# Five edits to the order of a one-core decoder trunk: a bias tile moved to another slot, and work queued behind query splits, a first cast and the last sums

## The chip, the cores and the metric

The kernel runs on one core of a Trainium2 chip. The metric is the device time of one execution in microseconds (us); lower is better. Five engines work side by side, each in its own order: TensorE (PE) multiplies, VectorE (DVE) and ScalarE (ACT) do elementwise work, GpSimd (POOL) does a little of it, SyncE (SP) mostly issues DMA transfers.

## The reference, cut to what matters

One layer of a decoder for 1024 prompt tokens and 64 sample tokens (8 sequences of 8), model width 1024, all in fp32:

```
mod = silu(c) @ ada_w + ada_b;  shift, scale, gate = split(mod, 3)
h   = rmsnorm(x, norm_g) * (1 + scale) + shift
z   = h @ w_in + b_in                      # a_u a_v a_g | b_q b_k b_v b_g | c_... | m_g
ya  = chunk_gmlp(a_u, a_v, ...) * silu(a_g)
q, k = rmsnorm(b_q, qn_g), rmsnorm(b_k, kn_g)          # per head of 64
yb  = sliding_window_attention(q, k, b_v, sinks) * silu(b_g)
yc  = mlstm(...) * silu(c_g)
merged = sum over br of sigmoid(m_g[br]) * (y[br] @ w_branch[br])
out = x + gate * (merged @ w_out)
```

## The kernel before

Each fp32 operand of a matmul is split into a high part (a cast to fp32r, on ScalarE) and a low part (operand minus high part, on VectorE), and three products are summed: high x high, high x low, low x high. So nearly every weight block costs a DMA, a cast on ScalarE and a subtraction on VectorE before TensorE may use it. The tokens are cut into nine tiles (eight of 128 prompt tokens, one of 64 sample tokens) or into two halves of 544.

The order within an engine is made by a planner that simulates the program: each engine's queue is fixed before the run, and an instruction that must wait holds up all behind it on that engine. `tc.issue_after(ins)` makes instructions of a block stand behind `ins` in the queue of `ins`'s engine; it sets an order and adds no semaphore. From the attention on, TensorE's queue is the program's order (`manual_schedule`). SBUF is handed out by name: `slot("m1", ...)` is a fixed region that passes from one user to the next, and a pool tile (`bt(...)`) takes memory that earlier phases used. A new user waits for the old one's last reader.

The phases, in order of time:

1. Start (to about 75 us): four blocks of the modulation are multiplied (`mod`, steps M0 to M3). Each ends in a copy of a PSUM bank to `msb` (ScalarE, L356), which small matmuls with `sel` then read. Then `hprep` makes the activations `hh`, `hlo`. Step P, the last, loads and splits the second weight slab (`load_pieces(1)`, four casts L124 and four subtractions L125); its VectorE part stands behind the last `modB` of M3.
2. Branch C (to about 353 us), whose results `hn[h]` lie in the slots m0 to m3, are gated there (L799) and stored (`dy<-hn`, on POOL's queue).
3. Attention (to about 600 us). `kv_tile` computes keys and values tile by tile; VectorE adds the bias tile `bkb` and so frees the PSUM bank (L942, L943). `bkb` lies in the memory of the later tile `Pp`. The first sums `t_first` (four times two subtractions, a sum and a split over 128x544) are issued among the kv tiles. A list of steps then runs the queries: `Prompt.q` computes the norms of three query tiles at a time (`q_stats`: squares L1001, row sums L1002, and on POOL a power L163) and then transposes and splits one tile (`q_transpose`: cast L1027, subtraction L1028); two steps later `s` does the logits and the softmax, two more later `p` transposes the probabilities `Sm`. Other products (queries, gMLP rows, gates) fill in. `t_second(k)` and `t_third(0)` make further sums; `mix(g)` is the last use of the slots y7, m5, y6, m0.
4. Products of halves (to about 1070 us): `items` is a list of pairs (prepare, run). `prepare` loads and splits a weight block up to LEAD = 5 items ahead, `run` multiplies. The first four are gMLP blocks of `plain`, (i, j) = (0,0), (0,1), (1,0), (1,1): its first run needs (0,0) and (0,1). `splits[n]` holds the cast and the subtraction of the n-th split made there. `last_gate`, `t_late(k)` and `t_in_place(k)` stand between them.
5. Projections and output. `proj` loads the earlier partial sum (`mprev<-dmg`, SP) and adds it; for f = 3 and 7 `m_split` splits the finished sum into `mh`, `ml` at once (L1643, L1644). The output product reads `mh`, `ml` and the output weights, loaded by `wo_load(0)` to `wo_load(3)` (each eight DMAs, four casts, four subtractions).

Of the kernel before, what the change touches and what calls it, by code (L numbers as in the profile page):

```python
# [8 lines left out]
F32 = mybir.dt.float32  # L9
# [18 lines left out]
HT = NT // 2  # L28
# [10 lines left out]
def trunk_kernel(ctx: ExitStack, tc: tile.TileContext, I, O):  # L39
# [197 lines left out]
    with tc.tile_pool(name="start", bufs=1, side="right", reuse_waits="tile") as st:  # L237
# [110 lines left out]
        def mod(j):  # L348
            pm = pk()
            for q in range(4):  # L350
                o = slice(256 * (q // 2), 256 * (q // 2) + 256)
                for kk in range(4):
                    mm(pm[32 * kk:32 * kk + 32, o], sT[:, 4 * (q % 2) + kk], ada_raw[j, q][:, 256 * kk:256 * kk + 256],
                       q % 2 == 0, q % 2 == 1)
            msb = st.tile([128, 512], F32, tag="msb", bufs=2, name="msb")
            S.copy(msb, pm)  # L356
            pc = pk()
            if j == 0:
                tr(pc[:, 128:160], Ra)
                V.tensor_copy(cols[:, CADA:CADA + 32], pc[:, 128:160])  # L360
                V.tensor_scalar(cols[:, CADA + 8:CADA + 16], cols[:, CADA + 8:CADA + 16], 1.0, None, ALU.add)
            for q in range(4):
                mm(pc[:, 16 * q:16 * q + 9], msb[:, 128 * q:128 * q + 128], sel, True, True)
            for d in range(2):
                k = 2 * j + d
                last["m"] = V.tensor_scalar(modA[:, k], pc[:, 16 * d:16 * d + 9], cols[:, CADA + 8 + k:CADA + 9 + k],
                                cols[:, CNG + k:CNG + k + 1], ALU.add, ALU.mult)
                V.tensor_scalar(modB[:, k], pc[:, 32 + 16 * d:32 + 16 * d + 9], cols[:, CADA + k:CADA + k + 1],
                                None, ALU.add)
# [37 lines left out]

        for step in STEPS.split():
            if step == "P":
                with tc.issue_after(last["m"].ins):  # L410
                    load_pieces(1, [None] * 3 + [st.tile([128, 528], F32, name="raw1")])
            elif step == "S":
                ps = pk()
                tr(ps[:, 0:68], R1)
                V.tensor_copy(cols[:, 0:CADA], ps[:, 0:CADA])
                V.tensor_copy(cols[:, CCB:100], ps[:, CADA:68])
            elif step[0] == "N":
                norm(int(step[1]))
            elif step[0] == "M":
                mod(int(step[1]))  # L420
            else:
                ci = int(step[2])
                for k in range(int(step[0]), int(step[1]) + 1):
                    hprep(k, ci)
                    for i in range(2 if ci < 2 else 1):
                        part(k, ci, i)
# [402 lines left out]
        t_split(x, to[0][:, c], to[1][:, c])  # L829
        TT[q, k] = to  # L830

    T4S = ("y6", "m0", "m4", "m1")

    kept = []
    keep = ExitStack()
# [2 lines left out]
    with tc.tile_pool(name="bph", bufs=1, side="right", reuse_waits="tile") as b1:  # L838
        def bt(shape, name, dt=F32, bufs=1, tag=None):
            return b1.tile(shape, dt, tag=tag or name, bufs=bufs, name=name)  # L840

        bkb = bt([128, 256], "bkb", tag="Pp")
        nc.sync.dma_start(bkb, b_in[:, 2048:2304].broadcast_to([128, 256]))
        qgb = bt([128, 64], "qgb")
        nc.sync.dma_start(qgb, I["swa_qnorm_g"].broadcast_to([128, 64]))
# [164 lines left out]
                    V.tensor_tensor(qr, qr, r3[:64, 2, 2 * i:2 * i + 2].unsqueeze(2).broadcast_to([64, 2, 64]), ALU.mult)  # L1010


        def q_transpose(g, n):
            tn = TILES[n][1]
            pq = pk()
            for i in range(2):
                tr(pq[:, tn * i:tn * i + tn], qraw[g][i][:tn, n])
            QT = bt([128, 2, 2, 128], "QT", F32R, bufs=3) if n < 8 else bt([128, 8, 4, 8], "QTs", F32R, bufs=2)
            for r in range(2):
                a, b = slice(64 * r, 64 * r + 64), slice(64 - 64 * r, 128 - 64 * r)  # L1020
                if n < 8:
                    src = pq[a, 0:256].rearrange("p (i t) -> p i t", i=2)
                    hi, lo = QT[a, :, r], QT[b, :, r]
                else:
                    src = pq[a, 0:128].rearrange("p (i b t) -> p b i t", i=2, b=8)
                    hi, lo = QT[a, :, r::2], QT[b, :, r::2]
                S.copy(hi, src)  # L1027
                V.tensor_tensor(lo, src, hi.bitcast(F32), ALU.subtract)  # L1028
            return QT.rearrange("p i r t -> p (i r t)")


# [2 lines left out]
        class Prompt:  # L1034
# [2 lines left out]

            def q(self):
                g, n = self.g, self.n
                if n % 3 == 0:  # L1040
                    q_stats(g, n)
                self.rr = r3s[g][:, n % 3]
                self.QT = q_transpose(g, n)
                if n == 7:
                    QTs[g] = q_transpose(g, 8)

# [185 lines left out]

        def t_second(k):
            x = slot(("m1", "m1", "y2", "y3")[k], [128, HT], name="tx")
            t_next(x, 6, k, k + 4, 1, 5, t_tile(("y0", "y1", "m2", "m3")[k]), slice(0, HT))

        def t_third(k):
            to = t_tile(T4S[k])
# [51 lines left out]
        def seq(*fs):  # L1290
# [2 lines left out]
        tail = {11: lambda: t_second(0), 13: lambda: t_second(1), 17: lambda: t_second(2),  # L1293
                18: seq(lambda: t_second(3), a_norm, lambda: a_scale(0)), 19: lambda: a_scale(1), 20: seq(lambda: a_scale(2), a_load),
                21: seq(lambda: a_scale(3), lambda: mix(0)), 22: seq(lambda: mix(1), lambda: mix(2)),
                23: lambda: mix(3), 24: lambda: t_third(0)}

        hl = next_slab()
        for n in range(9):
# [225 lines left out]
    def plain(cols2, final):  # L1525

        st = {}

        def prep(i, j):
            return w_split(raw_load(kv(w_in[:, cols2[i]:cols2[i] + 128])[:, 4 * j:4 * j + 4]))  # L1530

        def run(i, h):
            for j in range(2):
                c = part_(h, j)
                ps = bank()[:, :CUT[j][1]]
                for k in range(8):
                    three(ps, st[i, k // 4], k % 4, hh[k][:, c], hlo[k][:, c], k == 0, k == 7)
                x = tt(j)
                with tc.high_priority():
                    S.copy(x, ps)  # L1540
                final(i, h, j, x)

        def first(i, j, t):
            st[i, j] = t
            if j:
                run(i, 1)

        out = [(lambda i=i, j=j: prep(i, j), lambda t, i=i, j=j: first(i, j, t)) for i in range(2) for j in range(2)]
        return out + [(None, lambda _, i=i: run(i, 0)) for i in range(2)]

    Q7 = (1, 6, 7, 5, 3, 2, 4)
# [82 lines left out]
                V.tensor_tensor(yl[f][:, c], x, yh[f][:, c].bitcast(F32), ALU.subtract)  # L1634

    mh, ml = [None] * 8, [None] * 8

    def m_tiles(f):
        mh[f] = hp.tile([128, 1152], F32R, tag=f"hh{f}", name="mh")
        ml[f] = hp.tile([128, NT], F32R, tag=f"hl{f}", name="ml")  # L1640

    def m_split(f, c0, n, x):
        S.copy(mh[f][:, c0:c0 + n], x)  # L1643
        V.tensor_tensor(ml[f][:, c0:c0 + n], x, mh[f][:, c0:c0 + n].bitcast(F32), ALU.subtract)  # L1644
        if c0 + n == NT:
            S.copy(mh[f][:, NT:1152], ml[f][:, 1024:NT].bitcast(F32))

    def proj(n, f, Tt):
        br = ORDER_BR[n]

        def prep():
            return w_split(raw_load(kv(I["w_branch_" + "abc"[br]][0][:, 128 * f:128 * f + 128])))

        def run(t):
            if n == 2 and f % 4 == 3:
                m_tiles(f)
            for h in range(2):
                for j in range(2):
                    c = part_(h, j)
                    x = Tt[f, h, j]  # L1660
                    ps = bank()[:, :CUT[j][1]]
                    for k in range(4):
                        three(ps, t, k, yh[k][:, c], yl[k][:, c], k == 0, k == 3)
                    prev = None
                    if n:
                        prev = mp(CUT[j][1], "mprev")
                        nc.sync.dma_start(prev, dmg[f, :, c])
                    with tc.high_priority():
                        V.scalar_tensor_tensor(x, x, 1.0, ps, ALU.add, ALU.mult)
                    if n:  # L1670
                        V.tensor_tensor(x, x, prev, ALU.add)
                    if n == 2 and f % 4 == 3:
                        m_split(f, c.start, CUT[j][1], x)
                    else:
                        nc.sync.dma_start(dmg[f, :, c], x)

        items.append((prep, run))
# [37 lines left out]
    def last_gate(_):  # L1715
        c0, n, ps = kept[0]
        tz = y2[0].tile([128, 2, HT], F32, tag="yh1", name="tz")
        t, z = tz[:, 0, :n], tz[:, 1, :n]
        with tc.issue_after(splits[1][0]), tc.issue_after(splits[1][1]):
            S.activation(t, ps[:, :n], AF.Tanh, bias=bh[:, CBG + 3:CBG + 4], scale=0.5)  # L1720
            S.activation(z, ps[:, :n], AF.Identity, bias=cols[:, CBG + 3:CBG + 4], scale=1.0)
            V.scalar_tensor_tensor(z, t, 1.0, z, ALU.add, ALU.mult)
# [2 lines left out]
    it = [plain((0, 1024), gmlp_pair(0))]  # L1725
    it += [seven((128 * g, 1024 + 128 * g), (1, 2, 5, 6, 3, 7, 4) if g == 1 else Q7, gmlp_pair(g)) for g in range(1, 4)]
    gr = [x for g in range(4) for x in gate_rows(g)]
    items += [(None, last_gate)] + it[0][:2] + [behind(t_late, 1, 1)] + it[0][2:4] + [behind(t_late, 3, 2, 3), act(t_in_place, *((k,) for k in range(4)))] + it[0][4:]
    rest = it[1][:2] + [None] + it[1][2:3] + [None] + it[1][3:4] + [None] + it[1][4:5] + [None] + it[2][:1] + [None]
    rest += it[1][5:6] + [None] + it[1][6:] + [None] + it[2][1:2] + [None] + it[2][2:] + it[3]  # L1730
    items += [x or gr.pop(0) for x in rest]
# [33 lines left out]
        items[i][1](ready.pop(i))  # L1765


    gbc = slot("m6", [128, 1024], name="gbc")
    gbs = slot("m7", [128, 1024], name="gbs")
    nc.sync.dma_start(gbc, drow[0:1].broadcast_to([128, 1024]))  # L1770
# [23 lines left out]
    wo_load(0)  # L1794
    for i in range(4):
        if i < 3:
            wo_load(i + 1)
        c = slice(256 * i, 256 * i + 256)
        for n in tuple(range(9)) if i < 3 else (8,) + tuple(range(8)):
            t0, tn = TILES[n]  # L1800
# [55 lines left out]
```

## Time and profile before

| | |
|---|---|
| median of 3 runs | 1200.13 us (1199.48 to 1201.68) |
| profiled execution: its own time | 1201.65 us |
| profiled execution: span, first to last instruction | 1199.9 us |
| TensorE busy | 1160.6 us (97% of the span) |
| VectorE, ScalarE, GpSimd busy | 775.9, 489.0, 82.3 us |
| mean granted TensorE clock | 0.991 |

The span is shorter than the execution's own time by what lies before the first and after the last instruction. Busy time counts an engine's own instructions; matmuls overlap, so a busy TensorE need not be at its peak.

### The profile page before, as it was taken

The numbers are of one execution on the slowest core, as the hardware profiler recorded it, in microseconds if no ns is written. First come the engines' busy times: TensorE is split into PE (matmuls) and PEld (weight loads), VectorE is DVE, ScalarE is ACT, GpSimd is POOL, SyncE is SP. The second block draws the span as 40 slices with busy tenths as digits, with TensorE's granted clock in tenths as the row PEclk, the third lists the DMA queues.
The fourth block names the chain that finished last, engine by engine and source line by source line (L and its number), as shares of the span: only waits on it lengthen the run. The fifth ranks groups of instructions, "written<-read, shape, count | busy, mean of one in ns | idle before, by whom it ended". The sixth has DMA issues, their size and how long they took to land.

```text
span 1199.9 us, 23127 instructions
## 1 busy us (share of the span) xinstructions
PE 1160.6 (97%) x8924; PEld 1112.5 (93%) x8924; DVE 775.9 (65%) x1846; ACT 489.0 (41%) x1225; POOL 82.3 (7%) x111
## 2 busy tenths in 40 slices
PE   5899999999998999999999999999999999999998
PEld 2699999999988998888898999999999999998998
DVE  2577877655466678786588983645766676668333
ACT  4543455444332277887343441324332343335000
POOL 2100011012023210010000000000000000000000
PEclk9999999999998999999999999999999999999999
DMA  9721222222221210212234256423543354475322
GB/s 310 237 83 36 74 65 82 86 79 94 89 83 50 73 40 25 71 41 88 67 104 143 63 156 190 132 78 114 165 117 108 110 165 110 127 232 180 94 90 73
DMA packets 150772, 129.73 MB, mean 108 GB/s; under 512 B 13613, under 2 KB 140213, under 8 KB 150648
## 3 DMA queue, kind: packets, MB, share of 16 engines
q1 hardware_dynamic: 142984, 118.96, 33.4%
q0 software_dynamic: 2240, 7.08, 1.7%
q10 hardware_dynamic: 5440, 2.23, 0.7%
q8 instruction: 70, 1.15, 0.4%
q14 instruction: 38, 0.31, 0.1%
HBM read 99.39 MB, written 29.82 MB: 108 GB/s over the span
## 4 chain that ended last, share of the span: by engine, by line
PE 87%; DMA 5%; DVE 4%; SPq 3%; ACT 1%; issue 1%; ACTq 0%; DVEq 0%
PE pg L85 49%; PE pk L85 22%; PE pu L85 13%; PE pk L89 2%; DMA adaraw<-in_ada_w_dram 2%; SPq L251 1%; PE pu L89 1%; DMA mrow<-in_ada_b_dram 1%; DMA raw<-in_w_in_dram 1%; DMA mgr<-dmg 1%; DMA gbs<-drow 0%; SPq L267 0%; DMA raw<-in_w_out_dram 0%; DVE hl L125 0%; DVE wo L1395 0%
## 5 line engine op out<-in xcount | busy, mean ns | idle before, releaser
L85 PE MATMUL pg<-hl,hl 128*128 128x256 f32 (+3 forms) x904 | 279.2, 309 | 0.8 <-DVE hl L389 0.8
L85 PE MATMUL pg<-hh,hl 128*128 128x384 f32 (+1 forms) x912 | 238.1, 335 | 2.9 <-DVE hh L388 1.2
L85 PE MATMUL pg<-hl,hh 128*128 128x256 f32 (+1 forms) x1008 | 180.4, 286 | 5.3 <-DVE vB L943 5.3
L85 PEld LDWEIGHTS pg<-hl,hl 128*128 128x128 f32 x904 | 171.9, 190 | 3.9 <-DVE hl L389 1.7
L85 PEld LDWEIGHTS pg<-hh,hl 128*128 128x128 f32 x912 | 161.8, 189 | 7.4 <-DVE hh L388 2.6
L85 PEld LDWEIGHTS pg<-hl,hh 128*128 128x128 f32 x1008 | 152.5, 191 | 5.7 <-issue 5.4
L1394 ACT CAST prod<-raw 128x512 fp32r<-128x512 f32 x77 | 47.4, 619 | 118.6 <-PE pk L85 50.2
L85 PE MATMUL pg<-hh,prod 128*128 128x288 f32 (+1 forms) x408 | 86.9, 293 | 1.8 <-ACT prod L1394 1.6
L85 PE MATMUL pk<-hh,prod 128*128 128x256 f32 (+1 forms) x400 | 80.9, 285 | 0.0
L85 PEld LDWEIGHTS pg<-hh,prod 128*128 128x128 f32 x408 | 68.2, 191 | 2.7 <-ACT prod L1394 1.9
L1556 ACT ACTIVATE tt<-tt,bh 128x288 f32<-128x288 f32 x96 | 49.8, 522 | 47.1 <-DVE tt L1520 16.2
L1395 DVE TENSOR_TENSOR prod<-raw,prod 128x512 fp32r<-128x512 f32 x77 | 52.4, 685 | 24.9 <-ACT prod L1394 24.8
L85 PEld LDWEIGHTS pk<-hh,prod 128*128 128x128 f32 x400 | 65.1, 188 | 0.8 <-DVE tt L1512 0.4
L85 PE MATMUL pg<-yh,prod 128*128 128x288 f32 (+1 forms) x288 | 60.9, 290 | 0.0
L85 PE MATMUL pg<-hl,prod 128*128 128x288 f32 (+1 forms) x204 | 59.5, 292 | 0.0
L1394 ACT CAST prod<-comb 128x512 fp32r<-128x512 f32 x60 | 36.9, 614 | 54.2 <-PE pk L85 23.7
L85 PE MATMUL pk<-yh,prod 128*128 128x256 f32 (+1 forms) x288 | 58.7, 285 | 0.0
L85 PE MATMUL pu<-hh,prod 128*128 128x288 f32 (+1 forms) x280 | 57.7, 287 | 0.0
L85 PE MATMUL pk<-hl,prod 128*128 128x256 f32 (+1 forms) x200 | 56.8, 284 | 0.0
L85 PE MATMUL pk<-tc,prod 128*128 128x256 f32 (+1 forms) x408 | 56.2, 287 | 0.0
L85 PE MATMUL pg<-tc,prod 128*128 128x288 f32 (+1 forms) x396 | 55.7, 290 | 0.0
L85 PEld LDWEIGHTS pk<-tc,prod 128*128 128x128 f32 x408 | 52.7, 188 | 1.3 <-issue 0.9
(518 smaller groups left out, 2624.4 us busy)
## 6 DMA issues: line engine op xcount, KB each, us to landing
raw<-in_w_in_dram SPq DMA_DIRECT2D x124, 256.0 KB
adaraw<-in_ada_w_dram SPq DMA_DIRECT2D x16, 512.0 KB
stage<-dy SPq DMA_DIRECT2D x24, 272.0 KB
dmg<-tt SPq DMA_DIRECT2D x44, 144.0 KB
dmg<-tt SPq DMA_DIRECT2D x44, 128.0 KB
mprev<-dmg SPq DMA_DIRECT2D x32, 144.0 KB
xt<-in_x_prompt_dram SPq DMA_DIRECT2D x8, 512.0 KB
graw<-in_ada_w_dram SPq DMA_DIRECT2D x16, 256.0 KB
```

Of the source, the lines that this page charges most:

```text
L85: T.matmul(out, lhsT=lhsT, rhs=rhs, start=start, stop=stop)
L89: T.transpose(out, in_, ident[:k, :k])
L251: nc.sync.dma_start(raw.rearrange("p (k c) -> p k c", k=4), kv(ada_w[:, base:base + 256])[:, 4 * (q % 2):4 * (q % 2) + 4])
L1394: a = S.copy(t[:, 0], x)
L1395: b = V.tensor_tensor(t[:, 1], x, t[:, 0].bitcast(F32), ALU.subtract)
L1556: S.activation(x, x, AF.Tanh, bias=bh[:, b:b + 1], scale=0.5)
```

## The change

There are five edits.

- Start: the casts of the second slab (step P) stand behind M3's `msb` copy on ScalarE.
- Bias: `bkb` takes the slot m1 in place of `Pp`'s memory.
- Queries: `q_transpose` comes ahead of `q_stats`, whose VectorE instructions stand behind the latest query split, as do those of `t_second`.
- First weights: block (0,0) of `plain` is loaded and split in attention, behind `mix(3)`, in slot m0; `T4S` is reordered so that m0's sum is the last, and `t_late(3)` comes after the first block's last run. The numbers into `splits` drop by one, since one split less is made there.
- Output weights: the DMAs, casts and subtractions of `wo_load(1)` to `wo_load(3)` stand behind the last `mprev` load and the last `m_split` of the projections.

```diff
-            S.copy(msb, pm)
+            last["s"] = S.copy(msb, pm)
...
-                with tc.issue_after(last["m"].ins):
+                with tc.issue_after(last["m"].ins), tc.issue_after(last["s"].ins):
                     load_pieces(1, [None] * 3 + [st.tile([128, 528], F32, name="raw1")])
...
-    T4S = ("y6", "m0", "m4", "m1")
+    T4S = ("y6", "m4", "m1", "m0")
+    first = []
+
+    def first_weights():
+        raw = wp.tile([128, 528], F32, tag="raw", bufs=3, name="raw")
+        nc.sync.dma_start(raw[:, :512].rearrange("p (k c) -> p k c", k=4), kv(w_in[:, 0:128])[:, 0:4])
+        t = slot("m0", [128, 1040], F32R, name="pw")[:, 16:1040].rearrange("p (a c) -> p a c", a=2)
+        S.copy(t[:, 0], raw[:, :512])
+        V.tensor_tensor(t[:, 1], raw[:, :512], t[:, 0].bitcast(F32), ALU.subtract)
+        first.append(t)
...
-        bkb = bt([128, 256], "bkb", tag="Pp")
+        bkb = slot("m1", [128, 256], name="bkb")
...
-                V.tensor_tensor(lo, src, hi.bitcast(F32), ALU.subtract)
+                newq[0] = V.tensor_tensor(lo, src, hi.bitcast(F32), ALU.subtract).ins
...
                 g, n = self.g, self.n
+                self.QT = q_transpose(g, n)
                 if n % 3 == 0:
-                    q_stats(g, n)
+                    with tc.issue_after(newq[0]):
+                        q_stats(g, n)
                 self.rr = r3s[g][:, n % 3]
-                self.QT = q_transpose(g, n)
...
-            t_next(x, 6, k, k + 4, 1, 5, t_tile(("y0", "y1", "m2", "m3")[k]), slice(0, HT))
+            with tc.issue_after(newq[0]):
+                t_next(x, 6, k, k + 4, 1, 5, t_tile(("y0", "y1", "m2", "m3")[k]), slice(0, HT))
...
-                23: lambda: mix(3), 24: lambda: t_third(0)}
+                23: seq(lambda: mix(3), first_weights), 24: lambda: t_third(0)}
...
         def prep(i, j):
+            if not i and not j:
+                return first[0]
...
-        S.copy(mh[f][:, c0:c0 + n], x)
-        V.tensor_tensor(ml[f][:, c0:c0 + n], x, mh[f][:, c0:c0 + n].bitcast(F32), ALU.subtract)
+        lastm[1] = S.copy(mh[f][:, c0:c0 + n], x).ins
+        lastm[2] = V.tensor_tensor(ml[f][:, c0:c0 + n], x, mh[f][:, c0:c0 + n].bitcast(F32), ALU.subtract).ins
...
-                        nc.sync.dma_start(prev, dmg[f, :, c])
+                        lastm[0] = nc.sync.dma_start(prev, dmg[f, :, c]).ins
...
-    items += [(None, last_gate)] + it[0][:2] + [behind(t_late, 1, 1)] + it[0][2:4] + [behind(t_late, 3, 2, 3), act(t_in_place, *((k,) for k in range(4)))] + it[0][4:]
+    items += [(None, last_gate)] + it[0][:2] + [behind(t_late, 0, 1)] + it[0][2:4] + [behind(t_late, 2, 2), act(t_in_place, *((k,) for k in range(4)))] + it[0][4:5] + [act(t_late, (3,))] + it[0][5:]
...
+    lastp = list(lastm)
...
         if i < 3:
-            wo_load(i + 1)
+            with tc.issue_after(lastp[0]), tc.issue_after(lastp[1]), tc.issue_after(lastp[2]):
+                wo_load(i + 1)
```

## Rows read from the trace of the kernel before

**Rows 1.** The page: span, and PE's busy us (share) and instructions.

```profile
span 1199.9 us, 23127 instructions
PE   1160.6 (97%) x8924; PEld 1112.5 (93%) x8924; DVE 775.9 (65%) x1846; ACT 489.0 (41%) x1225; POOL 82.3 (7%) x111
```

**Rows 2.** PE's waits: releaser: us in total, times, longest us.

```profile
PE pg L85 <- DVE vB L943: 5.3, 1, 5.3
PE pk L85 <- ACT msb L356: 3.5, 3, 2.1
PE pg L85 <- ACT mh L1643: 2.7, 1, 2.7
PE pk L85 <- DVE QT L1028: 2.1, 1, 2.1
PE pk L89 <- DVE QT L1028: 1.8, 1, 1.8
PE pg L85 <- ACT prod L1394: 1.6, 1, 1.6
...
PE pu L89 <- ACT Sm L1075: 0.7, 1, 0.7
```

**Rows 3.** Windows: stretch, its us, PE PEld DVE ACT POOL busy, PEclk, DMA.

```profile
58.60:65.42 6.82, 6.23 (x22) 5.11 (x21) 6.79 (x27) 3.27 (x8) 0.00 (x0) 0.50 0.67 193
362.38:369.21 6.83, 5.34 (x25) 5.37 (x26) 5.54 (x20) 1.29 (x2) 6.66 (x9) 0.50 0.27 80
457.00:465.00 8.00, 5.89 (x48) 5.06 (x48) 6.54 (x18) 7.44 (x31) 2.47 (x2) 1.00 0.07 18
490.00:497.00 7.00, 5.25 (x44) 4.42 (x43) 6.43 (x19) 5.43 (x21) 2.94 (x2) 1.00 0.22 60
601.32:604.73 3.41, 3.41 (x15) 3.41 (x16) 2.89 (x6) 2.66 (x6) 0.54 (x1) 0.50 0.71 212
1099.66:1103.08 3.42, 3.25 (x15) 2.96 (x15) 3.11 (x9) 2.03 (x6) 0.00 (x0) 0.50 0.55 173
```

**Rows 4.** Timeline of ACT at M3's copy: start us, us, engine, line, instruction.

```profile
54.31 0.63 ACT L124 CAST hl<-raw 128x528 fp32r<-128x528 f32 x1 [0.69 <-DMA raw<-in_w_in_dram]
54.85 0.58 ACT L356 COPY msb<-pk 128x512 f32<-128x512 f32 x1
```

**Rows 5.** Timeline of DVE behind M3.

```profile
57.45 2.55 DVE L125 TENSOR_TENSOR hl<-raw,hl 128x528 fp32r<-128x528 f32 x4
```

**Rows 6.** Timeline of SP's queue where the bias is loaded.

```profile
356.80 0.46 SPq L843 DMA_DIRECT2D bkb<-in_b_in_dram  x1
```

**Rows 7.** Timeline of DVE at the first bias adds.

```profile
359.45 0.72 DVE L1226 TENSOR_TENSOR tx<-hh 128x544 f32<-128x544 f32 x1
...
363.25 0.27 DVE L942 TENSOR_TENSOR kn<-pg,bkb 128x128 f32<-128x128 f32 x1
```

**Rows 8.** Timeline of POOL: slot m1's store, and a mask.

```profile
300.22 0.57 POOL L800 DMA_DIRECT2D dy<-hn  x1
...
364.52 3.21 POOL L872 TENSOR_SCALAR_AFFINE_SELECT mN<-mN 32x128 f32<-32x128 f32 x1
```

**Rows 9.** Timeline of PE where the first mask is transposed.

```profile
372.44 0.27 PE L89 MATMUL pk<-ident,mT 128*128 128x128 f32 x1
```

**Rows 10.** Timeline of DVE at a late query split.

```profile
459.78 1.02 DVE L1001 TENSOR_TENSOR qs<-qraw 128x384 f32<-128x384 f32 x2
...
462.26 0.43 DVE L1028 TENSOR_TENSOR QT<-pk,QT 64x256 fp32r<-64x256 f32 x1
```

**Rows 11.** Tile rr (query norms): count, ns min/median/max, first to last start us.

```profile
L163 POOL TENSOR_TENSOR r<-rr,mhalf x6: 2265/2420/2743, 396.6 to 516.2; 128x12 f32<-128x12 f32 x6
```

**Rows 12.** Timeline of ACT behind the last attention copy.

```profile
599.84 1.14 ACT L1394 CAST prod<-raw 128x512 fp32r<-128x512 f32 x2 [0.44 <-ACT ys L1173]
```

**Rows 13.** Timeline of ACT at the last sums.

```profile
1098.39 0.62 ACT L1394 CAST wo<-raw 128x512 fp32r<-128x512 f32 x1 [1.53 <-DMA raw<-in_w_out_dram]
1098.91 0.43 ACT L1643 CAST mh<-tt 128x288 fp32r<-128x288 f32 x1
```

More of the change, by code (lines that the diff above doesn't have):

```diff
@@ L1010, in q_stats @@
                     V.tensor_tensor(qr, qr, r3[:64, 2, 2 * i:2 * i + 2].unsqueeze(2).broadcast_to([64, 2, 64]), ALU.mult)
+        newq = [None]
         def q_transpose(g, n):
@@ L1541, in run, with have @@
                 final(i, h, j, x)
-        def first(i, j, t):
+        def have(i, j, t):
             st[i, j] = t
@@ L1546, in first @@
                 run(i, 1)
-        out = [(lambda i=i, j=j: prep(i, j), lambda t, i=i, j=j: first(i, j, t)) for i in range(2) for j in range(2)]
+        out = [(lambda i=i, j=j: prep(i, j), lambda t, i=i, j=j: have(i, j, t)) for i in range(2) for j in range(2)]
         return out + [(None, lambda _, i=i: run(i, 0)) for i in range(2)]
@@ L1636, in trunk_kernel @@
     mh, ml = [None] * 8, [None] * 8
+    lastm = [None] * 3
     def m_tiles(f):
@@ L1718, in last_gate @@
         t, z = tz[:, 0, :n], tz[:, 1, :n]
-        with tc.issue_after(splits[1][0]), tc.issue_after(splits[1][1]):
+        with tc.issue_after(splits[0][0]), tc.issue_after(splits[0][1]):
             S.activation(t, ps[:, :n], AF.Tanh, bias=bh[:, CBG + 3:CBG + 4], scale=0.5)
```

## The prediction

> **What bounds the kernel now.** I read the page first. TensorE is busy 97% of the span [rows 1], so a faster VectorE or ScalarE is worth nothing in itself; only the 39 us in which TensorE does nothing, and the time in which it runs at its lower clock, can be had. Next I read TensorE's waits by releaser [rows 2], each being one or a few events, so each can be placed and looked at. The reader is to see that six lines make up nearly all the waiting after the first 20 us, and that each names another engine's instruction that was late. [...] Last, the timelines of the late engine in each place [rows 4 to 13], to see what stood in its queue ahead of the late instruction.
>
> What a fall costs is read from the busy column: work done at half clock takes twice its time, so half the busy time is lost. That is 6.23 / 2 = 3.1 us at 58.6, 5.34 / 2 = 2.7 at 362.4, 3.41 / 2 = 1.7 at 601.3 and 3.25 / 2 = 1.6 at 1099.7 [rows 3].
>
> **The clock: do the falls go with the waits?** Ahead of the falls at 601.3 and 1099.7 stand waits of 1.6 and 2.7 us, of the one at 362.4 a wait of 5.3 [rows 2, 3]. But two waits on the query splits, of 2.1 and 1.8 us, lie in windows whose clock stayed at 1.00 [rows 2, 3]: a wait does not always bring a fall, and what else counts there (many narrow matmuls, say) these rows do not tell. [...] I count the three falls that follow dense matmuls as gone with their waits, and keep the one at 58.6, where the work is narrow before and after (x22 matmuls in 6.8 us).
>
> **Start.** ScalarE's `msb` copies held TensorE three times for 3.5 us, the last time 2.1, so the other two took 0.7 each [rows 2]. The last copy stood behind a slab cast that itself waited for its DMA [rows 4]; four casts now follow it. The wait becomes 0.7: gain 1.4. The casts (4 x 0.63 = 2.5 us) are now ahead of the activations that make `hf`; late next would be VectorE's four subtractions, 2.55 us from 57.45 [rows 5], which start 1.4 earlier too, because the `modB` ahead of them does; the last cast (from about 54.0, so ended by 56.6) is in time for the last of them. No DMA moves. Bounds: 0 (VectorE keeps its pace) to 1.4 + 3.1.
>
> **Bias.** `bkb` is issued by SP at 356.80 [rows 6], behind weight loads, and VectorE's first add stands at 363.25, behind the first sums [rows 7]; TensorE lost 5.3 and 2.7 us. Slot m1 was stored by an issue at 300.22 [rows 8], over 40 us before the first add, so the one DMA (0.46 us of SP) can go early, past the weight loads, and the adds are ready as each tile ends. The sums (0.72 us an instruction) slide behind them; their results are needed only by later products. What is late next: TensorE would come to the masks 5.3 + 2.7 = 8.0 us earlier, at 364.4 in place of 372.44 [rows 9], but POOL ends `mN` at 364.52 + 3.21 = 367.7 [rows 8]. If the planner leaves the masks at their place, that gives back up to 3.3 us; if it lets kv tiles go first, nothing. I take half, 1.6: gain 6.4, bounds 8.0 and 2.0 (all given back, and a fall of the clock again).
>
> **Queries.** The splits that freed a bank late stood behind the norms: squares 1.02 us from 459.78, then two row sums, then the split at 462.26 [rows 10]. With the order turned, and the second sums (0.72 x 3 each) also behind, the split can come some 2 us earlier at both places; 3.9 us were lost [rows 2]. ScalarE's cast of the second half limits it too, and it has its own queue, so I count two thirds: gain 2.6, bounds 0 and 3.9. What is added is lateness of the norms: squares, row sums and a power of 2.4 us on POOL [rows 11] start after the split, by perhaps 1 to 2 us, at six places, and the softmax behind them. That is covered by the two steps between logits and the transposes of `Sm`: of 16 such groups only one held TensorE, by 0.7 us [rows 2]. Without that cover each would cost its 1 to 2 us. The second sums feed products of the next phase only.
>
> **First weights.** After the last attention copy ScalarE casts two blocks, 0.57 us each, from 599.84 [rows 12], and TensorE waits 1.6 us for the first [rows 2], so until about 600.4. With (0,0) split earlier, TensorE starts at about 600.4 - 1.6 = 598.8 on its first four groups, 12 matmuls, some 1.4 us at the upper clock (15 took 3.41 us at half [rows 3], so 0.11 each); the other block's cast ends at 599.84 + 0.57 = 600.4 and its low part some 0.7 later, which TensorE needs at about 600.5. About 0.5 is left. Gain 1.6 - 0.5 + 1.7 = 2.8, bounds 0 and 3.3. The moved step is one DMA of 256 KB past no load that waits, one cast and one subtraction in a stretch where VectorE and ScalarE have room; if they had none, it would cost its 0.6 us. `t_late(3)`, five instructions of about 0.7 us [rows 7], moves behind the first block's last run; its sum is used last of the seven products of the next block, several groups later, so nothing. The changed numbers into `splits` name the same instructions as before: nothing.
>
> **Output weights.** ScalarE casts `wo` at 1098.39 after 1.53 us of waiting for that block's DMA, and only then the `mh` that TensorE needs, at 1098.91 [rows 13]; 2.7 us lost, and 1.6 at half clock [rows 2, 3]. With 24 DMAs, 12 casts and 12 subtractions behind the last sum, the sums run as they come in. The added order holds up nothing that is wanted soon: block 1 of the output weights is needed after nine token tiles of the first block, some 20 us later, and its four casts and subtractions (0.6 and 0.7 us each) take about 3 us once the loads land. Were that cover gone, each block late would cost its 3 us. On SP the loads of `x` and the stores share the queue; they have slack of several banks. Gain 4.3, bounds 1.0 and 4.3.
>
> **The sum.** 1.4 + 6.4 + 2.6 + 2.8 + 4.3 = 17.5 us. Against it stands the planner: it draws up all queues anew, and the waits it left in the old plan without a reason that these edits touch were of 0.7 us or so [rows 2]. I take three such new ones, 2 us, bounds 0 and 6. That leaves 15.5. The profiled execution's own time, 1201.65, less 15.5 gives 1186.2; the median of the runs shown is 1.5 us lower (1200.13), so the forecast is 1184.6. All waits and falls gone would give 1200.1 - (1.4 + 3.1 + 8.0 + 3.9 + 3.3 + 4.3) = 1176.1.
>
> **Rivals.**
> - *The waits move.* TensorE comes to each stage sooner and meets the next late operand (masks behind POOL, the second block's low part, ScalarE's casts). For it: VectorE is busy 6.54 of 8 us and ScalarE 7.44 of 8 around 460 [rows 3]. Against it: the engines have 35% and 59% to spare over the span [rows 1]. Half of 17.5 stays: about 1191.
> - *The clock stays low.* The three falls remain although the waits shrink: 2.7 + 1.7 + 1.6 = 6.0 less, about 1190.5. The 0.50 at 58.6 in narrow work speaks for it, the 1.00 at 457 and 490 against.
> - *Norms come late: slower.* In place, the steps of attention. Each of the six norms and four second sums now queues behind a split that waits for ScalarE; if each held the softmax, and so TensorE, the whole gain of 15.5 is used up at 1.6 us a place, and at 2 us the kernel is at 1200.1 + 4.5 = about 1204.6. The power's own spread of 2.27 to 2.74 us [rows 11] shows that POOL is sometimes held. [...] Against it: only one wait on `Sm` in 16.
> - *Nothing comes of it.* The planner hoists none of the steps as meant, and the gain stays under 2.4 us (0.2%, about what a measurement of this kernel can tell from no change): about 1199.
>
> **How the numbers follow.** Forecast 0.50 (its own range 1179 to 1189), waits move 0.23, clock stays 0.14, norms late 0.06, nothing 0.07. Faster by over 0.2%: 0.50 + 0.23 + 0.14 = 0.87; within 0.2%: 0.07; slower: 0.06. The range takes in the forecast and both rivals of smaller gain, from near the sum of all waits to what is left when the waits move and some falls stay: 1177 to 1196.
>
> **What would show it.** Right: in the waits of TensorE the lines on `vB`, `mh` and `prod` are gone or under 0.5 us, `msb` sums to 2.1, `QT` is under 1.3; SP issues `bkb` before 350; the clock is 1.00 around where the kv tiles, the first blocks and the output start. Wrong: waits of over 1 us on masks, `wsr` or `kst` among the kv tiles; new waits on `Sm` or `QT` in attention; a wait on `wo` at a change of output block; or falls of the clock at places that have none now.

## The result, and the profile after

The changed kernel takes 1188.66 us (median of 6 runs, 1185.67 to 1192.66), the kernel before beside it 1200.14 (6 runs, 1199.48 to 1201.68): a ratio of 0.9906, 95% interval [0.9882, 0.993]. That is 11.5 us less; 15.5 were forecast, and the time lies 4.1 us above the forecast of 1184.6, inside the range. Launched again on another chip, it came to 0.989 [0.9873, 0.9907].

The profiled execution is the shortest of the six, 1185.67 us, so 16.0 below the profiled one of before (1201.65). The page of the kernel after, its head and part 1, answering to [rows 1]:

```profile
span 1184.0 us, 23111 instructions
PE 1154.9 (98%) x8924; PEld 1108.1 (94%) x8924; DVE 777.7 (66%) x1846; ACT 489.0 (41%) x1225; POOL 81.3 (7%) x111
```

TensorE idles 1184.0 - 1154.9 = 29.1 us instead of 39.3, and is busy 5.7 us less with the same 8924 matmuls. So 10.2 us come from waits and 5.7 from shorter busy time, which I put down to the clock: its mean went from 0.991 to 0.997. Which waits is seen in the waits of TensorE by releaser (us in total, times, longest us), answering to [rows 2]:

```profile
PE pk L89 <- ACT ts L1230: 3.7, 1, 3.7
PE pg L85 <- DVE hh L388: 2.3, 3, 1.1
PE pk L85 <- ACT msb L356: 2.1, 3, 0.7
PE pk L89 <- DVE KT L987: 1.2, 1, 1.2
PE pu L85 <- DVE tt L1518: 1.2, 1, 1.2
PE pk L89 <- DVE qraw L1020: 1.0, 1, 1.0
...
PE pg L85 <- DVE prod L1409: 0.2, 1, 0.2
```

The lines on `vB`, `mh` and `QT` are gone, `prod` is down from 1.6 to 0.2 and `msb` from 3.5 to 2.1. Three lines are new among the larger ones: 3.7 put down to `ts`, 1.0 for `qraw` and 1.2 for `KT`; and `hh` has grown from 1.2 us to 2.3. The windows with the granted clock, at the places of [rows 3] (all of them earlier now: by 2 us at the start, 9 at the first blocks, where TensorE begins at 591.94, and 12 at the output, where it begins at 1082.11) and at the one place where the clock now falls:

```profile
56.43:63.26 6.83, 5.77 (x34) 4.49 (x33) 6.83 (x26) 3.76 (x9) 0.00 (x0) 1.00 0.69 193
354.00:380.00 26.00, 24.78 (x210) 24.07 (x209) 23.18 (x69) 8.81 (x24) 11.85 (x17) 1.00 0.29 84
515.42:522.25 6.83, 6.19 (x22) 4.78 (x22) 3.12 (x14) 5.54 (x21) 2.57 (x3) 0.50 0.08 30
590.00:600.00 10.00, 9.80 (x75) 9.32 (x74) 6.98 (x13) 5.14 (x12) 0.54 (x1) 1.00 0.61 179
1081.00:1092.00 11.00, 11.00 (x96) 11.00 (x95) 8.96 (x20) 4.94 (x10) 0.00 (x0) 1.00 0.79 249
```

All four old falls of the clock are missing in this execution, even the one at the start that the forecast kept, and TensorE has 0.2 us of gap where the first blocks begin and none where the output begins. Against that stands a new fall, from 515.42 on; reckoned as in the prediction, half of its busy time is lost: 6.19 / 2 = 3.1 us. That half is an estimate and a little high: the 128x384 matmuls on `pg` start 0.32 us apart at 0.50 (three from 518.23 to 519.19) and 0.17 apart at 1.00 (six from 523.61 to 524.65). The fall goes with the 3.7 us wait. What that wait was for is read from the timelines of VectorE, GpSimd, ScalarE and TensorE ahead of it (start us, us, engine, line, instruction, and in brackets the idle time before it with the releaser):

```profile
509.16 1.03 DVE L1011 TENSOR_TENSOR qs<-qraw 128x384 f32<-128x384 f32 x2
510.11 1.00 DVE L1012 TENSOR_REDUCE rr<-qs 128x6 f32<-128x384 f32 x2
511.49 2.27 POOL L163 TENSOR_TENSOR r<-rr,mhalf 128x12 f32<-128x12 f32 x1
514.64 0.69 DVE L1075 TENSOR_REDUCE nm<-Sm 128x4 f32<-128x512 f32 x1
515.24 0.47 DVE L1228 TENSOR_TENSOR vn<-ts,avb 64x128 f32<-64x128 f32 x2
515.64 0.48 DVE L1020 TENSOR_TENSOR qraw<-qraw,r 64x128 f32<-64x128 f32 x2
515.76 0.19 ACT L1230 ACTIVATION_READ_ACCUMULATOR ts<-vn 64x1 f32 x1
516.06 0.47 PE L89 MATMUL pk<-ident,qraw 64*128 64x64 f32 x2 [3.72 <-ACT ts L1230]
```

The matmuls that wait are the transposes of query tile 8 (64x64), and they read `qraw`. `ts` on ScalarE (L1230) is the name that the profile gives: it ends at 515.95, just before they start, but they read nothing that it writes. What they do read is written by VectorE's L1020, whose first of two ends at about 515.9: by it `q_stats(g, 6)` scales tile 8 in place. That instruction needs the norms of tiles 6 to 8: squares, row sums, a power of 2.27 us on GpSimd, which ends at 513.76, and then its turn on VectorE behind L1075 and L1228. `q_stats(g, 6)` is issued in step 6 and tile 8 is transposed in step 7. The `qraw` line of 1.0 us is the same place for the first pair of heads, at 447.06, and there the profile names L1020 itself.

### The profile page after: what moved, and what is told of

It reads as the page before. It is cut to its first block, busy times and chain, and to the rows that moved or that the text cites. A ratio compares the mean times of both kernels' runs of the same rounds, so it can differ in the third digit from the quotient of the medians.

```text
span 1184.0 us, 23111 instructions
## 1 busy us (share of the span) xinstructions
PE 1154.9 (98%) x8924; PEld 1108.1 (94%) x8924; DVE 777.7 (66%) x1846; ACT 489.0 (41%) x1225; POOL 81.3 (7%) x111
## 4 chain that ended last, share of the span: by engine, by line
PE 85%; DMA 5%; DVE 4%; ACT 2%; issue 1%; SPq 1%; POOL 0%; ACTq 0%; DVEq 0%
PE pg L85 47%; PE pk L85 22%; PE pu L85 13%; PE pk L89 2%; DMA stage<-dy 2%; DMA raw<-in_w_in_dram 1%; DMA dy<-stage 1%; SPq L251 1%; ACT Sm L1080 1%; DVE hl L125 1%; PE pu L89 1%; DVE Sm L1072 0%; DVE nm L1075 0%; DVE QT L1040 0%; DVE rr L1012 0%
## 5 line engine op out<-in xcount | busy, mean ns | idle before, releaser
L85 PE MATMUL pg<-hl,hh 128*128 128x256 f32 (+1 forms) x1008 | 178.0, 283 | 0.0
L85 PE MATMUL pg<-hh,prod 128*128 128x288 f32 (+1 forms) x400 | 83.9, 289 | 0.2 <-DVE prod L1409 0.2
L85 PE MATMUL pk<-hh,prod 128*128 128x256 f32 (+1 forms) x384 | 78.1, 285 | 0.0
L85 PEld LDWEIGHTS pg<-hh,prod 128*128 128x128 f32 x400 | 65.8, 188 | 1.1 <-issue 0.4
L85 PEld LDWEIGHTS pk<-hh,prod 128*128 128x128 f32 x384 | 62.6, 188 | 0.8 <-DVE tt L1526 0.4
```

The lines of the kernel that those rows point to most:

```text
L85: T.matmul(out, lhsT=lhsT, rhs=rhs, start=start, stop=stop)
```

## The experiments

Theory A: each edit is worth the stall that it removes, except that the norms, now behind the splits, come too late for one reader that has only one step of cover, query tile 8. Rivals: late norms hold the softmax in general; the newly planned queues move the waits elsewhere; or the clock falls whatever the waits are. Every version was timed beside the kernel before on the same chip. "All edits but" means the kernel after with one part put back; "alone" the kernel before with one part put in.

**Norms of step 6 put back ahead of the transposes.**

```
                 if n == 6:
                     q_stats(g, n)
                 self.QT = q_transpose(g, n)
                 if n % 3 == 0 and n < 6:
                     with tc.issue_after(newq[0]):
                         q_stats(g, n)
```

> All five edits, but at n = 6 the norms keep their old place ahead of the query transposes (they are the ones that scale query tile 8, which the next step transposes). Theory A (the new waits of 1.0 and 3.7 us on the transposes of tile 8, and the fall of the clock at 515 that costs some 3 us, come from those norms standing one split later): both waits go, the profile has no fall there, and the profiled time is about 1185.7 - 7.7 = 1178. Theory B (the planner's new plan is simply fuller on VectorE in that stretch): waits of 1 to 4 us stand at the next late operand, and the time stays within 2 us of the changed kernel, 1184 to 1188.

Measured: 1187.12 us, ratio 0.9876 [0.9855, 0.9896], which is theory B's time. Both waits on tile 8 were gone, as theory A wanted, but a `QT` line came back, in the waits of TensorE:

```profile
PE pk L85 <- DVE QT L1040: 3.0, 2, 2.2
```

The longer of the two, 2.17 us at 522.81, stood ahead of a fall of 3.41 us. From the timelines of VectorE and ScalarE ahead of it:

```profile
506.24 1.00 DVE L1012 TENSOR_REDUCE rr<-qs 128x6 f32<-128x384 f32 x2
520.39 0.42 DVE L1040 TENSOR_TENSOR QT<-pk,QT 64x256 fp32r<-64x256 f32 x1 [1.08 <-ACT QT L1039]
520.90 0.57 ACT L1205 ACTIVATE zb<-pg,cols 128x384 f32<-128x384 f32 x1
521.58 0.37 ACT L1039 CAST QT<-pk 64x256 fp32r<-64x256 f32 x1
522.23 0.43 DVE L1040 TENSOR_TENSOR QT<-pk,QT 64x256 fp32r<-64x256 f32 x1
```

Step 6's norms did not hold this split: their row sums had ended by 507.3. VectorE sat idle 1.08 us until ScalarE had made its cast, and the second cast stood behind other work on ScalarE (`zb`, a gate). So the waits on tile 8 come from step 6's norms standing late, and with those waits gone another engine's queue was the next to be late. The interval takes in the second launch of the kernel after (0.989), so this run shows where the wait comes from, but no better version.

**All edits but the queries'.** `q`, `q_stats` and `t_second` as before; start, bias, first weights and output weights as after.

> The changed kernel without the queries edit (norms and second sums as before). Theory A: the old waits on the query splits, 2.1 and 1.8 us, are back and the new ones on tile 8 are gone, so it is some 3 to 4 us faster than the changed kernel: about 1181 to 1183. Theory B: the edit was worth its 2.6 us and more, so it is slower than the changed kernel, about 1188 to 1191.

Measured: 1187.79 us, 0.9889 [0.9864, 0.9914]. The two `QT` waits of before, 2.1 and 1.8 us, are there again, and nothing waits for tile 8. The ratio is that of the kernel after in its two launches (0.9906 and 0.989), so neither theory's difference is seen: on balance the queries edit as made brought nothing that can be measured. Theory A reckoned from the one profile of the kernel after, in which the fall at the start is missing; the profile here has that fall, and one behind the first `QT` wait.

**Second sums alone of the queries edit.** `q_stats` ahead of `q_transpose` as before, `t_second` behind `newq`.

> The changed kernel with only the second sums behind the query splits, the norms ahead of the transposes everywhere as before. Theory A: no wait on tile 8; part of the old 3.9 us on the splits is gone, since the first of the two late splits stood behind second sums and norms alike: about 1178 to 1182. Theory B: 1184 to 1190, with waits on splits or the softmax in other steps.

Measured: 1183.99 us, 0.9849 [0.9827, 0.9871]. TensorE waits for the splits 2.2 us in two waits instead of 3.9, and nothing waits for tile 8. All four runs (1182.90 to 1184.83) lie below all six of the version without the queries edit on this chip (1186.95 to 1193.68), so this half of the edit gains; the waits account for 1.7 of the 3.8 us between the medians, and the two intervals touch. The time lies between the two theories.

**The queries edit alone.**

> The kernel before with the queries edit alone. Theory A: 3.9 us of waits on the splits go, about 4.7 us on tile 8 come, with a fall of the clock in some executions: 1199 to 1204, not faster. Theory B: 1196 to 1198, faster by the 2.6 us forecast.

Measured: 1201.92 us, 0.9995 [0.9982, 1.0008]: nothing, to 0.2%. From the waits of TensorE of this version:

```profile
PE pk L89 <- ACT ts L1220: 3.7, 1, 3.7
...
PE pk L89 <- ACT pg L1220: 0.8, 1, 0.8
```

The tile 8 waits, 3.7 + 0.8 = 4.5 us, replace the 3.9 us on the splits [rows 2], without any other edit. They come with this edit alone, and need none of the others.

**The kernel after again, beside three single edits.** The bias edit alone is `bkb = slot("m1", ...)`; the first weights' is `first_weights`, `prep`, `T4S` and `behind(t_late, ...)`; the output weights' is `lastm` and `issue_after(lastp[...])`.

> The kernel after the change itself, again, as the partner on this chip of the three single edits below. Theory A (the edits act one by one, each is worth the stall that it removes, and the queries edit is worth nothing on balance): 11 to 12 us below the kernel before (ratio 0.990 to 0.991), and the single edits for the bias, the first weights and the output weights, with 1.4 for the start, add up to this gain within 2 us. Rival B (part of each gain is taken back elsewhere by the newly planned queues, so that single edits are not additive): the single edits add up to 3 us more or less than this gain. The wait of TensorE for the scaling of query tile 8 should be seen again at 3 to 4 us.

> The kernel before with the bias edit alone. Theory A: the wait on the copy of the bias into the first tile (5.3 us) and the half-clock stretch behind it (2.7 us) go, and a wait of 1.2 us for the key tile's split comes, as in all versions with this edit: 6.8 us less, ratio 0.994. My prediction's own term was 6.4. Rival B: the masks or the newly planned queues give more of it back: 2 to 4 us less, ratio 0.997 to 0.998.

> The kernel before with the edit of the first weights alone. Theory A: the wait for the first block (1.6 us) falls to about 0.2 and the half-clock stretch behind it (1.7 us) goes: 3 us less, ratio 0.9975 (predicted term: 2.8). Rival B: the wait moves to the second block or into the end of attention: 0 to 1 us less, ratio 0.999 to 1.000.

> The kernel before with the edit of the output weights alone. Theory A: the wait for the high part of the last sum (2.7 us with its small neighbours) and the half-clock stretch (1.6 us) go: 4.3 us less, ratio 0.9964. Rival B: TensorE waits instead for the output weights of block 1 or for the stores' queue: under 2 us less, ratio above 0.998.

**The start's edit alone:** `issue_after(last["s"].ins)` around `load_pieces`.

> The kernel before with the start's edit alone: the four casts behind the last msb copy. Theory A: the last msb wait falls from 2.1 us (1.5 to 3.0 in the executions seen) to 0.7, and the half-clock stretch near 58 us stays: 1 to 2 us less, ratio 0.9985 to 0.999, hardly to be told from 1. Rival C (the wait brings the half clock, which goes with it): 4 to 5 us less, ratio 0.996, and a clock of 1.00 from 50 to 65 us.

Measured, with the gain worked out from the ratio and the median of before on that chip (1201.98, and 1200.31 for the start):

| version | median us | ratio, 95% interval | gain, us |
|---|---|---|---|
| all edits | 1188.40 | 0.989 [0.9873, 0.9907] | 13.2 |
| bias | 1196.62 | 0.9955 [0.9939, 0.9971] | 5.4 |
| first weights | 1198.14 | 0.9966 [0.9954, 0.9978] | 4.1 |
| output weights | 1198.47 | 0.9968 [0.9954, 0.9981] | 3.8 |
| start | 1197.16 | 0.9977 [0.996, 0.9994] | 2.8 |

All edits together gained 13.2 us where 11 to 12 were expected, which is within the interval, with the waits on tile 8 there again (3.7 and 0.8 us). Reckoned as set down beforehand, with 1.4 for the start and nothing for the queries, the single edits come to 14.7, within 2 us of 13.2, as theory A has it. The five measured gains (with 2.8 for the start and 0.6 for the queries) sum to 16.7, 3.5 more. Each has an interval of 1.4 to 2 us to either side, so this does not show that they take from one another, nor that they don't. Each of the four is a gain by itself, at the place that the prediction named. The wait on `KT` of 1.2 us is in every version with the bias edit and in none without it: it is that edit's give-back.

The start is between its two theories: 2.8 us, where the shorter wait alone accounts for 1.4 and wait and fall together for 4.5. The fall near 58 us is in the profile of this version too, half as long as in [rows 3]:

```profile
55.00:63.00 8.00, 6.59 (x33) 5.05 (x33) 7.46 (x30) 5.45 (x11) 0.00 (x0) 0.79 0.69 229
```

**Tile 8 transposed two steps later.** The order of the change is kept, with all norms behind the splits; the line `QTs[g] = q_transpose(g, 8)` moves from `q` of step 7 to `s` of step 7, which runs two steps on, behind the logits.

```
-                if n == 7:
-                    QTs[g] = q_transpose(g, 8)
 ...
             def s(self):
 ...
+                if n == 7:
+                    QTs[g] = q_transpose(g, 8)
                 nm = bt([128, 4], "nm", bufs=2)
```

> The kernel after the change, with the norms still behind the transposes in all six steps, but the transposes of query tile 8 moved from the step right behind its norms to two steps later, behind that tile's logits. Nothing reads them before the sample steps. Theory A (the lateness of the norms hurts only where tile 8 is read one step later): both waits on the scaled tile 8 (0.96 and 3.72 us) go, and the stretch of 3.4 us lost at half clock behind the second: 4 to 8 us below the kernel after, so 1181 to 1185 us on a chip where the kernel before is at 1200 to 1202 (ratio 0.983 to 0.986). Rival N (norms that come late hold the softmax in general, and tile 8 is only where it shows first): waits of over 1 us for Sm or QT come up at other steps, and the ratio stays at 0.988 or more.

Measured: 1183.52 us (1181.42 to 1184.27, 4 runs), 0.9853 [0.9837, 0.987]; its interval lies wholly below both that of the second launch of the kernel after (0.9873 to 0.9907) and that of the first (0.9882 to 0.993). The page's part 1, and the window around the place:

```profile
PE 1155.2 (98%) x8924; PEld 1108.1 (94%) x8924; DVE 778.4 (66%) x1846; ACT 488.5 (41%) x1225; POOL 80.9 (7%) x111
```

```profile
57.69:64.52 6.83, 6.08 (x20) 5.14 (x21) 6.76 (x27) 2.90 (x8) 0.00 (x0) 0.50 0.70 193
500.00:530.00 30.00, 30.00 (x215) 26.72 (x214) 24.90 (x71) 27.18 (x97) 6.04 (x7) 1.00 0.25 72
```

TensorE is busy for all 30 us at a clock of 1.00 where the kernel after lost 3.7 and 3.1, though the norms run as late as there. From the waits of this version, whole lines:

```profile
PE pk L89 <- DVE KT L987: 1.2, 1, 1.2
PE pu L89 <- ACT Sm L1088: 1.2, 1, 1.2
```

`Sm` is the one wait that rival N may claim: 1.2 us at 546.79. It is one place among the 16 prompt steps, where the kernel before had one of 0.7 [rows 2], and the last of the six powers had ended at 515.6, 31 us before. Late norms in general are not what cost the time; the one short path was.

**The second sums alone, once more, beside it.**

> The version with all edits but the norms left ahead of the transposes as in the kernel before (the second sums behind the splits), once more, beside the version with tile 8 moved. If its lead over the kernel after was real: ratio to before 0.983 to 0.987 again, about 1184 us. If it was chance between launches: 0.988 to 0.990. Theory A expects the version with tile 8 moved to be within 2 us of it; rival N expects this one to be ahead by 4 us or more.

Measured: 1184.82 us, 0.987 [0.9853, 0.9886]. This version and the one with tile 8 moved beat the kernel before in every launch. The latter beats the kernel after; this one did so in its first launch, while the interval of its second overlaps both of the kernel after. Between the two, 1.3 us with overlapping intervals, the runs don't decide.

## Why the prediction was right or wrong

**What bounds it: right.** VectorE and ScalarE are as busy as before (777.7 and 489.0 us), and all that was won in the profiled execution is 10.2 us of TensorE's idle time and 5.7 of its clock. One reading was too strong: the six lines of [rows 2] called nearly all of the waiting after the first 20 us are 16.3 of the 22.9 us listed.

**Start: right in the wait, open in the fall.** `msb` sums to 2.1 as forecast, a gain of 1.4 (of which `hh` took back 0.5 in the kernel after, see below), and was at 0.7 for the last copy in all eight profiles of versions with this edit. The fall that I kept was in seven of them and missing in the profile of the kernel after alone, by which that execution is some 3.1 us shorter than its neighbours by [rows 3]; its median lies 3.0 above it. The version with this edit alone gained 2.8 [0.7, 4.8]: more than 1.4 cannot be excluded. The stretch at half clock there lasts 6.8 us in three and 10.2 in two of the five profiles without the edit, and 6.8 in six, 3.4 in one and none in one of the eight with it; that speaks for a shorter fall and does not settle it. That this fall stays while the other three go was my estimate: the profile after has none of the four, the other seven with this edit have this one.

**Bias: right in size, wrong in what gives some of it back.** Forecast 6.4; the trace gives 5.3 for the wait and 2.7 for the clock less 1.2 for `KT`, so 6.8; alone it measured 5.4 [3.5, 7.3]. SP issues `bkb` at 299.3. The masks held nobody: GpSimd made the last `mN` in 1.11 us, from 362.45, where it had taken 3.21 from 364.52 [rows 8]; why it was shorter is not shown. TensorE came to the masks at 363.85 in place of 372.44 [rows 9], and to `mN` itself at 364.06, 0.5 us after it was done, so with no wait: that the masks gave nothing back was a near thing. Late instead is the second split of the transposed keys, behind two slab subtractions, in VectorE's timeline:

```profile
375.46 1.28 DVE L125 TENSOR_TENSOR hl<-raw,hl 128x512 fp32r<-128x512 f32 x2
376.82 0.17 DVE L995 MEMSET qraw<- 64x128 f32 x1
377.02 0.29 DVE L987 TENSOR_TENSOR KT<-pk,KT 128x128 fp32r<-128x128 f32 x1
```

**Queries: here the prediction failed.** The step that failed is "That is covered by the two steps between logits and the transposes of Sm". It looked at one reader of the norms, the softmax, and for that one it held: the waits of the kernel after, shown down to 0.2 us, have no line on `Sm`. It missed the other reader, the in-place scaling of tile 8 (L1020), whose result the next step transposes. What I gave as the price without cover, 1 to 2 us a place, came out as 1.0 and 3.7, with 3.1 of clock behind it. So the trace takes 7.8 back from the 3.9 won on the splits, where +2.6 stood in the sum. That is -3.9 us in the profiled execution; as times, the edit alone was worth 0.6 [-1.0, 2.2]. With tile 8 moved, the trace has no line on `QT` and none on tile 8, so the 3.9 that I took as the upper bound are won there. The times agree (0.9853 against 0.9889 without the queries edit, some 4.3 us) but don't show it: the intervals overlap, and the chips differ (the kernel before at 1200.31 on the one, 1202.27 on the other). The other limit that I named, ScalarE's cast, is what held the split in the version with step 6's norms put back.

**First weights: right.** Forecast 2.8; the trace shows 1.6 + 1.7 = 3.3, the upper bound, since the 0.5 feared on the second block did not come: its 0.2 stood there before too (last line below). Alone it measured 4.1 [2.6, 5.5].

**Output weights: right.** Forecast 4.3; the wait (2.7) and the fall (1.6) are both gone, and no wait on `wo` came at a change of block; alone 3.8 [2.3, 5.5].

**New waits of the plan: put down at 2 us, on balance none.** Some lines of the kernel before:

```profile
PE pg L85 <- DVE hh L388: 1.2, 2, 1.0
PE pu L85 <- DVE tt L1504: 0.8, 1, 0.8
PE pg L85 <- ACT gsb L1699: 0.7, 1, 0.7
PE pg L85 <- DVE ff L533: 0.6, 1, 0.6
PE pg L85 <- DVE prod L1395: 0.2, 1, 0.2
```

Apart from tile 8 and `KT`, which belong to the queries and the bias, `tt` has grown from 0.8 to 1.2, and `hh` has a third wait, of 1.1 us at the start, where `ff` stood with 0.6. Against these, the lines of 0.7 on `gsb` and on `Sm` [rows 2] are gone. With the queries at zero, the sum would have been 17.5 - 2.6 - 2 = 12.9, beside 11.5 and 13.2 measured.

**The number: near in the profiled execution by luck.** It came 16.0 lower where 15.5 were forecast. The queries fell 6.5 us short (-3.9 for +2.6); this was made up by the fall at the start, 3.1 us, which is missing in this profile alone, by the 2 us for new waits that did not come, and by small waits that went. The medians, 11.5 and 13.2 lower, are what the change is worth.

**The rivals.** "The clock stays low" is wrong for the three falls that I counted as gone: none of the seven profiles of versions with these three edits has one there. "The waits move" names what happened, for one operand, `KT`. "Norms come late" had the right mechanism in the wrong place, at the price of one edit and not of the whole gain. The longer powers, which I took as a sign that GpSimd is sometimes held, can be seen beside VectorE's work in the timelines of VectorE and GpSimd of the kernel after:

```profile
401.32 0.69 DVE L125 TENSOR_TENSOR hl<-raw,hl 128x512 fp32r<-128x512 f32 x1
401.43 2.71 POOL L163 TENSOR_TENSOR r<-rr,mhalf 128x12 f32<-128x12 f32 x1
402.35 1.28 DVE L125 TENSOR_TENSOR hl<-raw,hl 128x512 fp32r<-128x512 f32 x2
...
486.23 0.73 DVE L828 TENSOR_TENSOR tx<-tx,hl 128x544 f32<-128x544 f32 x1
486.34 2.74 POOL L163 TENSOR_TENSOR r<-rr,mhalf 128x12 f32<-128x12 f32 x1
...
511.14 0.69 DVE L1100 SCALAR_TENSOR_TENSOR Pp<-mcT,pu 128x512 f32<-128x512 f32 x1
511.49 2.27 POOL L163 TENSOR_TENSOR r<-rr,mhalf 128x12 f32<-128x12 f32 x1
```

The power takes 2.71 and 2.74 us where a slab subtraction and a second sum had begun on VectorE 0.11 us before it, and 2.27 where the `Pp<-mcT,pu` had begun 0.35 us before it. What makes the difference is not shown. It is 0.45 us, less than the 0.7 us of the VectorE instruction, and it had no part in the lateness of tile 8, whose power took 2.27. The subtractions were not longer for it: two more began at 402.35, within the power that ended at 404.14, and took 0.64 us each, as did the two ahead of `KT` at 375.46. So this piece of the rival is small.

## What to carry to other kernels

When work is moved behind something, list every reader of its results and the shortest path from it to the next matmul; the reader with the least cover sets the price, not the typical one. Here one small in-place scaling with one step of cover cost as much as the edit brought, and moving its reader two steps on, with the edit untouched, gave it back. And where the profile names a releaser, see whether the waiting instruction reads what it wrote: another, ended at the same moment, may be the one.

## What the runs showed of the hardware

The same wait stands beside a fall of the clock in one profiled execution and without one in another; each version has one profile. The wait of 5.3 us on `vB` had one in all five profiles that have the wait, the 3.7 us for tile 8 in all three. The 1.57 us on `prod` had one in three of five (the kernel before, bias alone, output weights alone), the `mh` wait of 2.2 to 2.8 in four of five, the 2.1 us on `QT` in two of six, though not in the kernel before [rows 3], and the 1.75 us on the second `QT` in none of six. Two windows of the version with the start's edit alone, around the waits on `prod` and `mh`, and one of the version with the bias alone around the first `QT`:

```profile
597.00:602.00 5.00, 3.61 (x25) 3.38 (x26) 3.68 (x6) 3.92 (x9) 0.54 (x1) 1.00 0.46 131
1093.00:1099.00 6.00, 3.97 (x32) 3.77 (x33) 5.18 (x13) 3.38 (x8) 0.00 (x0) 1.00 0.69 207
```

```profile
457.00:465.00 8.00, 6.94 (x46) 6.97 (x47) 4.90 (x15) 3.32 (x13) 2.46 (x2) 0.79 0.06 16
```

So the clock terms of the sum, 2.7, 1.7 and 1.6, were what one execution showed; for the waits of 1.57 to 2.8 us here they are chances, and a single profile neither proves nor excludes them. The same kernel differs from run to run too: over 25 executions of the kernel before on one chip the mean granted clock went from 0.984 to 0.993.
